# Expert stage of a two-layer backbone: full and small experts in alternating blocks, on one core

## The chip, the cores and the metric

The kernel runs on one core of a Trainium2 chip. The metric is the device time in microseconds, as the median of several executions. A profile of one execution shows where the time goes. The engines are TensorE (PE in the profile, with its weight loads as PEld), VectorE (DVE), ScalarE (ACT), GpSimd (POOL) and SyncE (SP), whose queue issues nearly all loads from HBM.

## The reference, cut to what matters

256 latent and 256 context tokens of width 1024 go through two layers, each with a mixer (gated linear attention, differential attention, neighbourhood attention) and a channel mixer. In the second layer the channel mixer is a mixture of eight experts, computed for the 256 latent tokens. This is the part that changes:

```python
def swiglu(h, wg, wu, wd):
    return (jax.nn.silu(h @ wg) * (h @ wu)) @ wd

def moe_swiglu(h, w_router, wg, wu, wd):
    ...
    logits = (t @ w_router).astype(jnp.float32)
    top_v, top_i = lax.top_k(logits, TOP_K)          # 2 of 8
    top_w = jax.nn.softmax(top_v, axis=-1)
    gates = jnp.sum(jax.nn.one_hot(top_i, N_EXPERTS, dtype=jnp.float32) * top_w[..., None], axis=1)
    y = jnp.zeros_like(t)
    for e in range(N_EXPERTS):
        y = y + gates[:, e:e + 1].astype(t.dtype) * swiglu(t, wg[e], wu[e], wd[e])
    return y.reshape(shp)
```

Everything is float32. An expert has wg and wu of 1024 x 3584 and wd of 3584 x 1024, 44 MB together; all eight are 352 MB, and every one is read once.

## The kernel before, in words

The kernel runs the first layer, then the second layer's mixer, then the expert stage, then the final norm. The tokens of an expert are gathered with one-hot matrices (S) by PE, and its results are scattered back into xtk, the token-major sum, in the same way. Experts are ordered by their token count (`order_experts`, `order_index`); expert 0 stays first, so that its loads can start early. The first four in this order (NBIG) are full: they take up to 128 tokens. The last four are small: up to 64 tokens. A branch at the end does the rest if some expert has more, and is not taken here.

An expert goes in NJ = 7 blocks of 512 hidden columns. A block loads six pieces of 1 MB: two halves of gate, two halves of up, two halves of the down weights of the block before. Between gate and up PE transposes the block before's activations (`g_T`).

*Full experts* (`expert`): the weights are split into a high and a low part (`convert`, lines 789 to 804): ScalarE copies to the rounded format float32r, VectorE subtracts. Each product is then three products (`mm3`: high-high, high-low, low-high) of 128 x 512 columns. Split pieces live in three pairs of buffers (mpr twice, mpc once), used in turn. The raw piece is free once it is split.

*Small experts* (`expert_small`): the raw float32 weights are used as they are (`load_raw`). Two products with 64 token columns each stand side by side in the two halves of the array and of one PSUM bank (gate and up, or the two halves of the down columns). The raw piece is free once PE has used it.

*The ring of slots*: each load takes the next slot of a list (`slot32`). `first` gives the slots of the first loads, `ring` the order after that, and `until` the load number from which a slot is taken out, because its memory then serves as something else. Some slots are memory of tiles that are needed only later (xh, xl: the gathered tokens of experts 2 and 3, xt: xtk, y: the split scatter operand, xc: part of xT). Five slots are left after load 62. SP issues loads in order, and each waits until its slot is free.

*Order*: the Tile framework records the program, fixes the order of instructions on each engine by a priority close to program order, and inserts the semaphores. `plan` hangs smaller jobs behind certain blocks: the ordering of the experts, gathers, one-hot matrices, rows of broadcast vectors, the addition of x. All full experts run first, then all small ones; the `tail` of an expert (its last down product and scatter) runs in the first block of the next.

*PSUM*: pgu has two banks each for the tags pg and pu, pdn one each for pd0 and pd1, pmt two for transposes, gathers and scatters. A small expert uses pg and pu in turn and one of pd0 and pd1.

*Scatter of a full expert* (`scatter_half`, line 1163): y is scaled, split into high and low (ScalarE, VectorE), and two float32r products per token half add up in PSUM.

Of the kernel before, what the change touches and what calls it, by code (L numbers as in the profile page):

```python
# [89 lines left out]
def hybrid_backbone_kernel(  # L90
# [679 lines left out]
    n_load = [0]  # L770

# [81 lines left out]
    tab = const.tile([P, TAB_C], F32, name="tab")  # L853
    nc.sync.dma_start(tab, k_tab[:, 0:TAB_C])
    mskF = const.tile([P, 2, P], U32, name="mskF")
# [31 lines left out]
    for k in range(KD):  # L887
# [10 lines left out]
    pgu = pool("pgu", 2, space=PSUM)  # L898
# [15 lines left out]
    S = mp.tile([P, 2, NE, P], F32R, name="S")  # L914
# [24 lines left out]
    for q in range(2):  # L939
        for t in range(2):  # L940
            pt = pgu.tile([P, 512], F32, tag="pg" if t == 0 else "pu", name="pht")
# [24 lines left out]
    def onehots(e0, n, pos):  # L966
        return tt(S[:, :, e0:e0 + n, :], tb("iota", tab2, TAB_C).rearrange("p (a b n) -> p a b n", a=1, b=1).to_broadcast([P, 2, n, P]),
           pos[:, :, e0:e0 + n].unsqueeze(3).to_broadcast([P, 2, n, P]), ALU.is_equal)

    def onehots_twice():  # L970
        n = NE - NBIG
        it = tb("iota", tab2, TAB_C)[:, 0:P // 2].rearrange("p (a b n) -> p a b n", a=1, b=1).to_broadcast([P, n, 2, P // 2])
        for t in range(2):
            tt(S[:, t, NBIG:NE, :].rearrange("p e (d n) -> p e d n", d=2), it,
               posp[:, t, NBIG:NE].rearrange("p (e a b) -> p e a b", a=1, b=1).to_broadcast([P, n, 2, P // 2]), ALU.is_equal)

    tc.keep_in_program_order(onehots(0, 1, posm))
# [92 lines left out]
    def load_e(dram, kk, n):  # L1070
        i = n_load[0]
        n_load[0] += 1
        wh, wl = ready[i] if i in ready else convert(i, slot32(i), dram, kk, n, (mpr, mpr, mpc)[i % 3])
        return wh.rearrange("p (k n) -> p k n", n=n), wl.rearrange("p (k n) -> p k n", n=n)
# [19 lines left out]
    def gather_small():  # L1094
        n = (NE - NBIG) * (P // 2)
        xs = mp.tile([P, KD, n], F32, tag="xeH1", name="xs")
        for m in range(0, KD, 2):
            pt = bank(pmt, "pga")
            for mi in range(2):
                for i, (src, t) in enumerate(((htH, 0), (htL, 0), (htH, 1), (htL, 1))):  # L1100
                    mm(pt[:, mi * n:(mi + 1) * n], lhsT=src[:, t, (m + mi) * P:(m + mi + 1) * P],
                       rhs=S[:, t, NBIG:NE, 0:P // 2], start=i == 0, stop=i == 3)
# [3 lines left out]
    def gate_up(w_ap, xe, j, tag):  # L1106
        ps = pgu.tile([P, 512], F32, tag=tag, name=tag)
        for half in range(2):
            w = load_e(w_ap[half * 512:(half + 1) * 512, j * 512:(j + 1) * 512].rearrange("(k p) n -> p k n", p=P), 4, 512)
# [5 lines left out]
    def act_mul(pg, pu):  # L1115
        g = mp2.tile([P, 512], F32, tag="eg", name="eg", bufs=2)
# [15 lines left out]
    NJ = FE // 512  # L1132

    def down(w_ap, gt, j, pds):
        for half in range(2):
            w = load_e(w_ap[j * 512 + half * 256:j * 512 + (half + 1) * 256, :].rearrange("(k p) n -> p k n", p=P), 2, D)
# [7 lines left out]
    def down_cols(w_ap, gt, pds, o):  # L1144
        r0 = (NJ - 1) * 512
        w = load_e(w_ap[r0:r0 + 512, o * 512:(o + 1) * 512].rearrange("(k p) n -> p k n", p=P), 4, 512)
        for q in range(4):
            mm3(pds[o], (gt[0][:, q, :], gt[1][:, q, :]), (w[0][:, q, :], w[1][:, q, :]), False, q == 3)

    def scatter_pre(Sf, gate_col):  # L1150
        pt = bank(pmt, "pst")
        for t in range(2):
            nc.tensor.transpose(pt[:, t * P:(t + 1) * P], f32(Sf(t)), ident)
        for t in range(2):
            mm(pt[:, 256:257], lhsT=f32(Sf(t)), rhs=gate_col(t), start=t == 0, stop=t == 1)
        ST = mp2.tile([P, 256], F32R, tag="ST", name="ST", bufs=2)
# [3 lines left out]
        return ST, gs, mp2.tile([P, 2, D], F32R, tag="y", name="yHL")  # L1160

    def scatter_half(sc, pds, o, first=False):
        ST, gs, yHL = sc
        yo = part(y32, o)
        cs = slice(o * 512, (o + 1) * 512)
        yH, yL = yHL[:, 0, cs], yHL[:, 1, cs]
# [12 lines left out]
    def expert(xe, wg, wu, wd, Sf, gate_col, tail, hooks=None, first=False, end=None):  # L1179
        pds = None  # L1180
        prev = None
        for j in range(NJ):
            pg = gate_up(wg, xe, j, "pg")
# [4 lines left out]
            pu = gate_up(wu, xe, j, "pu")  # L1188
            g = act_mul(pg, pu)
            if prev is not None:  # L1190
                if pds is None:
                    pds = [pdn.tile([P, 512], F32, tag=f"pd{o}", name="pd") for o in range(2)]
                down(wd, gt, j - 1, pds)
# [3 lines left out]
            for f in (hooks or {}).get(j, ()):  # L1197
                f()
# [5 lines left out]
        def t1():  # L1204
            if end:
                tc.keep_in_program_order(nc.scalar.preload_act_table_set(LN_EXP))
                sc = scatter_pre(Sf, gate_col)
                new_xg()
                for o in range(2):
                    down_cols(wd, last[0], pds, o)  # L1210
                    scatter_half(sc, pds, o)
                    end(o)
                return
            down(wd, last[0], NJ - 1, pds)
# [3 lines left out]
        return t0, t1  # L1218

# [8 lines left out]
    def expert_small(xs, wg, wu, wd, e, tail, hooks, end=None):  # L1228
# [4 lines left out]
        def g_Ts(g):  # L1233
# [3 lines left out]
            gt = mp2.tile([P, 4, H], F32, tag="gth", name="gts", bufs=2)  # L1237
# [3 lines left out]
        def down_s(gt, j):  # L1241
            if pd[0] is None:
                pd[0] = pdn.tile([P, 512], F32, tag=f"pd{e % 2}", name="pds")
# [9 lines left out]
        for j in range(NJ):  # L1253
            ps = pgu.tile([P, 512], F32, tag=("pg", "pu")[j % 2], name="pgs")
# [13 lines left out]
            g = mp2.tile([P, 512], F32, tag="eg", name="eg", bufs=2)  # L1268
# [7 lines left out]
            for f in (hooks or {}).get(j, ()):  # L1276
                f()
# [5 lines left out]
        def t1():  # L1283
# [3 lines left out]
            down_s(last[0], NJ - 1)  # L1287
            pt = bank(pmt, "pst")
            for t in range(2):
                nc.tensor.transpose(pt[:, t * P:(t + 1) * P], f32(S[:, t, e, :]), ident)  # L1290
            for t in range(2):
                mm(pt[:, 256:257], lhsT=f32(S[:, t, e, :]), rhs=gatp[:, t, e:e + 1], start=t == 0, stop=t == 1)
# [22 lines left out]
    def new_xg():  # L1315
        nonlocal xg
        xg = mp.tile([P, 2, D], F32, tag="xeH0", name="xg")
# [24 lines left out]
    def gather_at(e, n, xe, o=0):  # L1342
        return gather(lambda t: S[:, t, e:e + n, :].rearrange("p e n -> p (e n)"), n * P, xe, o)
# [3 lines left out]
    gather_at(0, 1, x01)  # L1347

    def gather_pair():
        xes[2] = gather_at(2, 2, xe_tiles(0))  # L1350
# [4 lines left out]
    def stack_ga2():  # L1355
        for o in range(2):
# [3 lines left out]
    plan = {(0, 1): [order_experts], (0, 2): [order_index, lambda: onehots(1, 1, posp)], (0, 4): [lambda: gather_at(1, 1, x01, P), load_order],  # L1360
            (0, 6): [lambda: row_bc(ga2b, lambda k: modT[1][:, 40 + k, 0:1])],
# [77 lines left out]
```

## Time and profile before

| | us |
|---|---|
| median of 3 runs (1972.12 to 1978.58) | 1977.36 |
| the profiled execution | 1977.44 |
| its span, first to last instruction | 1975.6 |
| PE busy | 1828.8 (93%) |
| DVE busy | 980.6 (50%) |
| ACT busy | 758.3 (38%) |

The page's slices show the two halves of the expert stage. Each digit is the busy share of a fortieth of the span (49.4 us) in tenths; the expert stage begins near slice 20.

```profile
PE   7999999999999999999899999999999878787886
DVE  5574554633333345755678888988984000010101
ACT  4424454422222234245466777667762000000001
PEclk9999999999999999999899999999999999989998
DMA  9664242342344244633579889999998999999996
GB/s 306 214 173 131 75 143 88 127 129 70 102 131 158 78 126 156 165 116 125 202 283 329 291 292 340 338 349 359 347 339 288 394 394 388 388 366 392 388 388 253
```

From slice 31 on VectorE and ScalarE are nearly idle, PE is below nine tenths, and the DMA moves more than before. Busy times of overlapped products count once; a product's own duration includes the overlap with its neighbours, so the pace of PE is read from the distance of starts.

### The profile page before, as it was taken

The numbers are of one execution on the slowest core, as the hardware profiler recorded it, in microseconds if no ns is written. First come the engines' busy times: TensorE is split into PE (matmuls) and PEld (weight loads), VectorE is DVE, ScalarE is ACT, GpSimd is POOL, SyncE is SP. The second block draws the span as 40 slices with busy tenths as digits, with TensorE's granted clock in tenths as the row PEclk, the third lists the DMA queues.
The fourth block names the chain that finished last, engine by engine and source line by source line (L and its number), as shares of the span: only waits on it lengthen the run. The fifth ranks groups of instructions, "written<-read, shape, count | busy, mean of one in ns | idle before, by whom it ended". The sixth has DMA issues, their size and how long they took to land.

```text
span 1975.6 us, 23201 instructions
## 1 busy us (share of the span) xinstructions
PE 1828.8 (93%) x9152; PEld 1255.2 (64%) x9152; DVE 980.6 (50%) x1296; ACT 758.3 (38%) x967; POOL 46.6 (2%) x75
## 2 busy tenths in 40 slices
PE   7999999999999999999899999999999878787886
PEld 4856766778877878677687878878784222222221
DVE  5574554633333345755678888988984000010101
ACT  4424454422222234245466777667762000000001
POOL 1030000000000000300000000000000000000000
PEclk9999999999999999999899999999999999989998
DMA  9664242342344244633579889999998999999996
GB/s 306 214 173 131 75 143 88 127 129 70 102 131 158 78 126 156 165 116 125 202 283 329 291 292 340 338 349 359 347 339 288 394 394 388 388 366 392 388 388 253
DMA packets 286113, 480.04 MB, mean 243 GB/s; under 512 B 11246, under 2 KB 141612, under 8 KB 285996
## 3 DMA queue, kind: packets, MB, share of 16 engines
q1 hardware_dynamic: 283488, 474.19, 68.2%
q0 software_dynamic: 1312, 2.62, 0.9%
q10 hardware_dynamic: 1196, 1.66, 0.3%
q8 instruction: 74, 1.21, 0.3%
q14 instruction: 43, 0.35, 0.1%
HBM read 477.39 MB, written 1.05 MB: 242 GB/s over the span
## 4 chain that ended last, share of the span: by engine, by line
PE 75%; DMA 13%; DVE 6%; ACT 3%; issue 2%; POOL 0%; DVEq 0%; ACTq 0%; POOLq 0%
DMA e<-in_w_moe_up_dram 12%; PE pd L1141 8%; PE pgs L1261 7%; PE pu L150 3%; PE pds L1249 3%; PE pu L151 3%; PE pg L149 3%; PE pu L149 3%; PE pg L150 3%; PE pg L151 3%; PE psg L149 2%; PE psg L150 2%; PE psg L151 2%; PE psu L149 2%; PE psu L150 2%; PE psd L149 2%
## 5 line engine op out<-in xcount | busy, mean ns | idle before, releaser
L803 DVE TENSOR_TENSOR el<-e,eh 128x2048 fp32r<-128x2048 f32 (+1 forms) x173 | 375.7, 2190 | 50.1 <-ACT eh L802 49.4
L802 ACT ACTIVATE eh<-e 128x2048 fp32r<-128x2048 f32 (+1 forms) x173 | 316.3, 1837 | 95.7 <-PE pu L151 33.7
L1261 PE MATMUL pgs<-e,xs 128*64 128x512 f32 x896 | 244.7, 623 | 75.1 <-DMA e<-in_w_moe_up_dram 69.8
L1261 PEld LDWEIGHTS pgs<-e,xs 128*64 128x64 f32 x896 | 70.2, 141 | 235.1 <-DMA e<-in_w_moe_up_dram 110.4
L142 ACT ACTIVATE wh<-w 128x2048 fp32r<-128x2048 f32 (+2 forms) x70 | 125.4, 1791 | 205.6 <-issue 78.6
L143 DVE TENSOR_TENSOR wl<-w,wh 128x2048 fp32r<-128x2048 f32 (+2 forms) x70 | 149.6, 2138 | 99.1 <-ACT wh L142 99.1
L1270 DVE TENSOR_TENSOR eg<-eg,pgs 64x512 f32<-64x512 f32 x28 | 19.3, 690 | 359.7 <-ACT eg L1269 359.7
L1269 ACT ACTIVATE eg<-pgs 64x512 f32<-64x512 f32 x28 | 16.5, 590 | 372.2 <-PE pgs L1261 372.2
L1249 PE MATMUL pds<-e,gts 128*64 128x512 f32 x448 | 127.6, 600 | 1.4 <-DMA e<-in_w_moe_down_dram 1.4
L149 PE MATMUL pg<-eh,xeH 128*128 128x512 f32 x224 | 89.9, 402 | 0.6 <-ACT eh L802 0.6
L150 PE MATMUL pg<-el,xeH 128*128 128x512 f32 x224 | 90.0, 402 | 0.0
L150 PE MATMUL pu<-el,xeH 128*128 128x512 f32 x224 | 89.3, 399 | 0.7 <-DVE el L803 0.6
L149 PE MATMUL pu<-eh,xeH 128*128 128x512 f32 x224 | 89.7, 401 | 0.0
L149 PE MATMUL psp<-hH,wh 128*128 128x512 f32 (+1 forms) x224 | 86.4, 390 | 3.1 <-ACT hH L274 3.0
L151 PE MATMUL pg<-eh,xeL 128*128 128x512 f32 x224 | 89.0, 397 | 0.0
L149 PE MATMUL psq<-wh,hH 128*128 128x256 f32 x304 | 88.7, 292 | 0.0
L151 PE MATMUL pu<-eh,xeL 128*128 128x512 f32 x224 | 88.5, 395 | 0.0
L150 PE MATMUL psq<-wl,hH 128*128 128x256 f32 x304 | 87.7, 289 | 0.0
L151 PE MATMUL psq<-wh,hL 128*128 128x256 f32 x304 | 87.4, 287 | 0.0
L150 PE MATMUL psp<-hL,wh 128*128 128x512 f32 (+1 forms) x224 | 85.8, 383 | 0.0
L151 PE MATMUL psp<-hH,wl 128*128 128x512 f32 (+1 forms) x224 | 85.2, 381 | 0.0
L1141 PE MATMUL pd<-el,gth 128*128 128x512 f32 x224 | 71.5, 400 | 1.6 <-DVE el L803 1.6
(504 smaller groups left out, 3436.3 us busy)
## 6 DMA issues: line engine op xcount, KB each, us to landing
e<-in_w_moe_gate_dram SPq DMA_DIRECT2D x111, 1024.0 KB, 7.8
e<-in_w_moe_up_dram SPq DMA_DIRECT2D x111, 1024.0 KB, 7.7
e<-in_w_moe_down_dram SPq DMA_DIRECT2D x111, 1024.0 KB, 7.6
wmod<-in_w_mod_dram SPq DMA_DIRECT2D x96, 512.0 KB, 5.4
w<-in_w_in_dram SPq DMA_DIRECT2D x24, 1024.0 KB, 8.0
w<-in_w_ffn_gate_dram SPq DMA_DIRECT2D x11, 1024.0 KB, 5.9
w<-in_w_ffn_up_dram SPq DMA_DIRECT2D x11, 1024.0 KB, 5.1
w<-in_w_out_dram SPq DMA_DIRECT2D x8, 1024.0 KB, 5.3
```

What stands on the lines that cost most here:

```text
L142: act(wh[:, :m], w32[:, :m], AF.Copy)
L143: tt(wl[:, :m], w32[:, :m], f32(wh[:, :m]), ALU.subtract)
L149: mm(ps, lhsT=sh, rhs=mh, start=first, stop=False)
L150: mm(ps, lhsT=sh, rhs=ml, start=False, stop=False)
L151: mm(ps, lhsT=sl, rhs=mh, start=False, stop=last)
L802: act(h3[:, b], w[:, b], AF.Copy)
L803: tt(l3[:, b], w[:, b], f32(h3[:, b]), ALU.subtract)
L1141: mm(pds[o], lhsT=gt[sh][:, q, :], rhs=w[mh][:, k, o * 512:(o + 1) * 512], start=a and j == 0 and q == 0, stop=z and j == NJ - 1 and q == 3)
L1249: mm(pd[0][H * o:H * o + H, :], lhsT=gt[:, q, :], rhs=w[:, k, o * 512:(o + 1) * 512], start=j == 0 and q == 0, stop=j == NJ - 1 and q == 3 ...
L1261: mm(ps[H * o:H * o + H, :], lhsT=xv[:, kk, :], rhs=ws[o][:, k, :], start=kk == 0, stop=kk == KD - 1, skip_group_check=True)
L1269: act(g[0:H], ps[0:H], AF.Silu)
L1270: tt(g[0:H], g[0:H], ps[H:P], ALU.mult)
```

## The change

- Full and small blocks alternate. `full_ones` and `small_ones` are generators that yield after each block; a loop runs one full block, then one small block, the small ones starting LAG = 4 blocks later. So four full blocks come first, 24 pairs follow, and four small blocks come last.
- `Weights` keeps the list of a full expert's loads through all four experts. After each full block it issues and splits AHEAD = 3 loads of the next one, ahead of the small block's loads in program order.
- The ring has a new slot v, and y stays in it: eight slots are left after load 42.
- The memory comes from the one-hot matrices, now built per expert (`onehot`, tile S1, two buffers) instead of for all eight, from the split scatter operand, from the buffers of eg, and from tab and mskF, which move from the pool const to a pool that is closed before the expert stage.
- Experts 2 and 3 are gathered one by one into the halves of experts 0 and 1 (x01), instead of together.
- A full expert's scatter multiplies the float32 y in one product instead of its two halves in two.
- PSUM: pgu has one bank each for pg, pu and the small experts' ps; pdn one each for pd0, pd1 and the small experts' pds.
- The jobs of `plan` hang behind blocks by number (`after`).

```diff
-    tab = const.tile([P, TAB_C], F32, name="tab")
+    tabp = big.enter_context(tc.tile_pool(name="tabp", bufs=1))
+    tab = tabp.tile([P, TAB_C], F32, name="tab")
...
-    pgu = pool("pgu", 2, space=PSUM)
+    pgu = pool("pgu", 1, space=PSUM)
...
+             "v": lambda: mp2.tile([P, 2048], F32, tag="v32", name="e32"),
...
-    first = ["r0", "r1", "r2", "w", "c", "r0", "r1", "xh", "xl", "xt", "y", "r2", "xc"]
-    ring = ["w", "c", "r0", "r1", "xh", "xl", "xt", "y", "r2", "xc"]
-    until = {"xc": 36, "xt": 42, "y": 42, "xh": 62, "xl": 62}
+    first = ["r0", "r1", "r2", "w", "c", "r0", "r1", "xh", "xl", "xt", "y", "v", "r2", "xc"]
+    ring = ["w", "c", "r0", "r1", "xh", "xl", "xt", "y", "v", "r2", "xc"]
+    until = {"xc": 26, "xt": 42, "xh": 22}
...
+    def onehot(pos, e, n=P):
+        S = mp2.tile([P, 2, P], F32R, tag="S1", name="S", bufs=2)
...
+    AHEAD = 3
...
+    class Weights:
+        def __init__(self, experts):
+            self.todo, self.got = [], []
+            for i, (wg, wu, wd) in enumerate(experts):
+                for j in range(NJ):
+                    for w_ap in (wg, wu):
+                        self.todo += [(w_ap, j, h) for h in range(2)]
+                    if j or i:
+                        self.todo += [((wd if j else experts[i - 1][2]), (j - 1) % NJ, h + 2) for h in range(2)]
+            self.todo += [(experts[-1][2], NJ - 1, h + 2) for h in range(2)]
+        def fetch(self, n):
+            while self.todo and len(self.got) < n:
+                w_ap, j, h = self.todo.pop(0)
...
+                self.got.append(load_e(ap.rearrange("(k p) n -> p k n", p=P), kk, m))
+        def next(self):
+            self.fetch(1)
+            return self.got.pop(0)
...
     def scatter_half(sc, pds, o, first=False):
...
-        act(half(yH), yo, AF.Copy)
-        tt(half(yL), yo, half(f32(yH)), ALU.subtract)
         for t in range(2):
             py = bank(pmt, "py")
-            mm(py, lhsT=ST[:, t * P:(t + 1) * P], rhs=yH, start=True, stop=False)
-            mm(py, lhsT=ST[:, t * P:(t + 1) * P], rhs=yL, start=False, stop=True)
+            mm(py, lhsT=ST[:, t * P:(t + 1) * P], rhs=yo, start=True, stop=True)
...
     def expert(...)
...
             prev = g
+            ws.fetch(AHEAD)
+            yield
...
+    LAG = 4
...
+    after = {0: [order_experts], 1: [order_index], 3: [gather_rest, load_order],
+             4: [lambda: row_bc(ga2b, lambda k: modT[1][:, 40 + k, 0:1])],
+             5: [lambda: gather_at(1, x01, P)],
+             8: [add_x], 9: [stack_ga2], 10: [lambda: gather_at(2, x01, 0)], 17: [lambda: gather_at(3, x01, P)],
+             16: [lambda: row_bc(gfb, lambda k: gfT[:, k:k + 1])]}
+    bigs, smalls = full_ones(), small_ones()
+    for i in range(NBIG * NJ + LAG):
+        next(bigs, None)
+        if i >= LAG:
+            next(smalls, None)
+        for f in after.get(i, ()):
+            f()
+    next(smalls, None)
     finish()
```

## Rows read from the trace of the kernel before

**Rows 1.** Windows: stretch, length, busy PE, PEld, DVE, ACT, POOL; clock, DMA share, GB/s.

```profile
1250.00:1300.00 50.00, 49.92 (x226) 40.05 (x225) 46.37 (x33) 34.74 (x24) 0.00 (x0) 1.00 0.97 345
1400.00:1450.00 50.00, 49.98 (x231) 40.77 (x230) 41.54 (x23) 35.74 (x25) 0.00 (x0) 1.00 1.00 358
1550.00:1600.00 50.00, 39.56 (x166) 12.45 (x166) 2.92 (x5) 2.53 (x5) 0.00 (x0) 1.00 1.04 394
```

**Rows 2.** Chain of waits in order of time: start us, length us, what.

```profile
1031.52 5.45 PE pd L1141 x24
1048.61 5.47 PE pd L1141 x24
1065.72 5.48 PE pd L1141 x24
1088.65 5.45 PE pd L1141 x24
1587.75 3.22 PE pgs L1261 x13
1593.15 10.53 DMA e<-in_w_moe_up_dram
1603.72 3.22 PE pgs L1261 x13
1948.65 8.75 DMA e<-in_w_moe_down_dram
```

**Rows 3.** What SP's queue waited for: us in total, times, longest us.

```profile
SPq L796 <- DVE el L803: 380.7, 140, 16.5
SPq L1225 <- PE pgs L1261: 247.9, 101, 10.5
```

**Rows 4.** Timeline of PE's weight loads and transposes in a small block.

```profile
1572.28 0.14 PEld L1261 LDWEIGHTS pgs<-e,xs 128*64 128x64 f32 x2 [0.28 <-issue]
1572.71 0.14 PEld L1261 LDWEIGHTS pgs<-e,xs 128*64 128x64 f32 x2 [0.28 <-issue]
1577.09 0.46 PE L1236 MATMUL pgt<-ident,eg 64*128 64x64 f32 x4
```

**Rows 5.** Groups by line, from 1000 us on: busy us, mean ns, idle before.

```profile
L803 DVE TENSOR_TENSOR el<-e,eh 128x2048 fp32r<-128x2048 f32 (+1 forms) x165 | 366.1, 2237 | 44.7 <-ACT eh L802 44.0
L1261 PE MATMUL pgs<-e,xs 128*64 128x512 f32 x896 | 244.7, 623 | 75.1 <-DMA e<-in_w_moe_up_dram 69.8 <-DMA e<-in_w_moe_gate_dram 5.1
L1249 PE MATMUL pds<-e,gts 128*64 128x512 f32 x448 | 127.6, 600 | 1.4 <-DMA e<-in_w_moe_down_dram 1.4
L802 ACT ACTIVATE eh<-e 128x2048 fp32r<-128x2048 f32 (+1 forms) x163 | 306.1, 1885 | 90.3 <-PE pu L151 33.7 <-PE pd L1141 30.6 <-PE pg L151 22.8
```

**Rows 6.** Shorter windows within the full experts, columns as in rows 1.

```profile
1050.00:1070.00 20.00, 20.00 (x90) 16.30 (x90) 18.81 (x13) 14.56 (x10) 0.00 (x0) 1.00 1.05 384
1382.00:1386.00 4.00, 4.00 (x19) 3.25 (x18) 3.77 (x4) 2.52 (x3) 0.00 (x0) 1.00 1.02 340
```

**Rows 7.** Loads of the page: size, median us from issue to landing.

```profile
e<-in_w_moe_up_dram SPq DMA_DIRECT2D x111, 1024.0 KB, 7.7
```

**Rows 8.** Timelines of SP and PE, and tile tab: min/median/max ns, first start.

```profile
32.64 2.86 SPq L854 DMA_DIRECT2D tab<-in_k_tab_dram x1
50.71 1.06 PE L229 MATMUL psmod<-wmod,Sz 128*32 128x256 f32 x14
L440 DVE TENSOR_TENSOR gu<-psu,tab x16: 681/684/692, 93.8 to 816.1; 128x512 f32<-128x512 f32 x16
```

**Rows 9.** PE's timeline where full experts give way to small ones.

```profile
1506.81 0.73 PE L1141 MATMUL pd<-eh,gth 128*128 128x512 f32 x2 [2.48 <-ACT eh L802]
1509.13 1.22 PE L1141 MATMUL pd<-el,gth 128*128 128x512 f32 x2 [1.59 <-DVE el L803]
1511.01 1.05 PE L1141 MATMUL pd<-eh,gth 128*128 128x512 f32 x2
```

**Rows 10.** The window around that place.

```profile
1491.00:1530.00 39.00, 34.92 (x130) 15.67 (x128) 12.58 (x16) 7.02 (x8) 0.00 (x0) 0.91 0.75 272
```

More of the change, by code (lines that the diff above doesn't have):

```diff
@@ L770, in hybrid_backbone_kernel @@
     n_load = [0]
+    n_conv = [0]
     wr = tab2 = None
@@ L1130, in g_T, with down @@
         return gh, gl
-    NJ = FE // 512
-    def down(w_ap, gt, j, pds):
+    def down(ws, gt, j, pds):
         for half in range(2):
-            w = load_e(w_ap[j * 512 + half * 256:j * 512 + (half + 1) * 256, :].rearrange("(k p) n -> p k n", p=P), 2, D)
+            w = ws.next()
             for k in range(2):
@@ L1177, in scatter_half, with expert @@
                 tt(xtk[:, t, cs], xtk[:, t, cs], py, ALU.add)
-    def expert(xe, wg, wu, wd, Sf, gate_col, tail, hooks=None, first=False, end=None):
+    def expert(xe, ws, Sf, gate_col, tail, first=False):
         pds = None
@@ L1204, in t1 @@
         def t1():
[L1205 to L1214, printed above, removed]
+            down(ws, last[0], NJ - 1, pds)
             sc = scatter_pre(Sf, gate_col)
@@ L1218, in expert, with run_expert @@
         return t0, t1
+    def run_expert(*args):
+        g = expert(*args)
+        while True:
+            try:
+                next(g)
+            except StopIteration as stop:
+                return stop.value
     def load_raw(dram, kk, n):
@@ L1226, in load_raw, with expert_small @@
         return wv
-    def expert_small(xs, wg, wu, wd, e, tail, hooks, end=None):
+    def expert_small(xs, wg, wu, wd, e, tail, end=None):
         H = P // 2
@@ L1275, in expert_small @@
             prev = g
-            for f in (hooks or {}).get(j, ()):
-                f()
+            yield
         last = []
@@ L1366, in hybrid_backbone_kernel @@
-    tail = None
-    for e in range(NE):
-        if e == 0:
-            ws = [w[0, 0] for w in (wm_g, wm_u, wm_d)]
-        else:
-            ws = [w[0, ds(which[e], 1)].rearrange("o a b -> (o a) b") for w in (wm_g, wm_u, wm_d)]
-        hooks = {j: f for (ee, j), f in plan.items() if ee == e}
-        if e >= NBIG:
-            tail = expert_small(xes[NBIG], *ws, e, tail, hooks, square if e == NE - 1 else None)
-            continue
-        xe, h = (x01, e * P) if e < 2 else (xes[2], (e - 2) * P)
-        xv = (xe[0][:, :, h:h + P], xe[1][:, :, h:h + P])
-        gt_ = gates if e == 0 else gatp
-        tail = expert(xv, *ws, lambda t, e=e: S[:, t, e, :], lambda t, e=e, g=gt_: g[:, t, e:e + 1], tail, hooks, e == 0)
@@ L1380, in hybrid_backbone_kernel, with weights, full_ones @@
-    tail[0]()
-    tail[1]()
+    LAG = 4
+    def weights(e):
+        if e == 0:
+            return [w[0, 0] for w in (wm_g, wm_u, wm_d)]
+        return [w[0, ds(which[e], 1)].rearrange("o a b -> (o a) b") for w in (wm_g, wm_u, wm_d)]
+    def full_ones():
+        tail = None
+        ws = Weights([[lambda e=e, i=i: weights(e)[i] for i in range(3)] for e in range(NBIG)])
+        for e in range(NBIG):
+            h = e % 2 * P
+            xv = (x01[0][:, :, h:h + P], x01[1][:, :, h:h + P])
+            gt_, ps_ = (gates, posm) if e == 0 else (gatp, posp)
+            tail = yield from expert(xv, ws, lambda e=e, p=ps_: onehot(p, e)[0], lambda t, e=e, g=gt_: g[:, t, e:e + 1], tail, e == 0)
+        tail[0]()
+        tail[1]()
@@ new lines, in small_ones @@
+    def small_ones():
+        tail = None
+        for e in range(NBIG, NE):
+            tail = yield from expert_small(xes[NBIG], *weights(e), e, tail, square if e == NE - 1 else None)
+        tail[0]()
+        tail[1]()
+    after = {0: [order_experts], 1: [order_index], 3: [gather_rest, load_order],
[3 more added lines that the diff above has]
+             16: [lambda: row_bc(gfb, lambda k: gfT[:, k:k + 1])]}
```

100 lines of the change are left out of this document (46 added, 54 removed).

## The prediction, made before the result was known

> **What bounds the kernel now.** I read the slices of the page first, then the windows of the last half, the chain of waits, the queue's own waits and the groups by line. The expert stage begins at about 990 us and has two halves. In the first, four full experts run in 28 blocks: PE is busy 49.9 to 50 us of every 50, VectorE 42 to 46, and the DMA delivers 345 to 358 GB/s [rows 1]. In the second, four small experts run in 28 blocks: PE is busy 40 of 50, VectorE 3, and the DMA is full at 394 GB/s [rows 1]. The chain says the same: a full block comes every 17.09 us (1031.52 to 1048.61, the down products of two neighbours) with no wait in it, a small block every 15.96 us (1587.75 to 1603.72, the gate and up products) with a DMA wait in each [rows 2]. Both kinds load six pieces of 1 MB, so a piece takes 2.85 us where PE sets the pace and 2.66 us where the DMA does. SP's queue waits on VectorE's split in the first half and on PE's products in the second [rows 3]: there the loads wait for a slot, since the first half cannot use more and the second has only five slots left. So the first half lacks PE, the second lacks DMA, and neither lends its spare to the other. The clock was granted at 2.4 GHz through the first half.
>
> **What a round costs after the change.** A round is one full and one small block. PE in the full block: 17.1 us. PE in the small block: weight loads come in twos 0.43 us apart where nothing holds them [rows 4]; 896 and 448 products in 28 blocks [rows 5] are 32 and 16 each, so 16 x 0.43 + 8 x 0.43 = 10.3 us, and 0.5 for four transposes: 10.8 us. Together 27.9 us. DMA: 12 pieces, at 2.66 us 31.9 us. VectorE: six splits of 2.24 us [rows 5] and four shorter operations of about 0.7: 16.2 us; ScalarE less. So a round is bound by the DMA, with 4 us of PE to spare, and the stage is 336 pieces at the DMA's pace. Before, only 28 of the 56 blocks ran at it.
>
> Do eight slots keep the queue full? In a round 12 pieces pass 8 slots, so at 2.70 us a piece a slot may be held 21.6 us from issue to release. I walked one round slot by slot: a piece lands 2.70 after the one before; a full piece is split 4.1 us after landing (ScalarE 1.9, VectorE 2.2, [rows 5]), and only when the piece three before it has been used, since there are three pairs of split buffers; a small piece is freed when PE has used it. From landing to release that is about 10.6 us for a full piece and 5 for a small one, 8 in the mean, which leaves 13 us from issue to landing; the page's median landing is 7.7 [rows 7]. So the queue holds about two pieces to spare, and short PE stalls (up to about 5 us) do not reach the DMA. The three pieces of the next full block that are split ahead of the small block change nothing in this sum: they let PE begin the full block without the 4.1 us of a split, which PE has to spare. They add one wait: the third of these splits cannot begin before PE has ended the full block, and behind it on ScalarE stand the small block's copies and Silu. PE first needs those 7 us into the small block, the split is through after 4.1, so nobody waits for them.
>
> **The rate.** The trace of before never shows the mix. The nearest rows: with PE and VectorE both full, but several pieces queued (share 1.05), 20 us gave 384 GB/s; a short window with a share of 1.02 gave only 340, right after the queue had run low [rows 6]. The small half gave 394. Bounds: 2.66 us (small blocks) and 2.85 us (full blocks). I take 2.70 us (388 GB/s), between the 384 of a full queue beside full engines, which this ring keeps, and the 394 beside small blocks.
>
> **The sum.** Up to the fourth full block nothing is interleaved and PE sets the pace as before: its down products end at 1048.61 + 5.47 = 1054 us. 22 pieces are used by then, and with nine slots (eight, and xtk's until piece 42) and three split ahead 34 have landed by about 1061. The ring is full while the small gather runs, so I let the DMA idle 7 us: next landing at 1071. From there 301 pieces x 2.70 = 813 us: 1884. The gather of expert 1 (1065.72 to 1088.65, 22.9 us between down products instead of 17.1) can drain the ring once more: +4. The small half of before had 28 x 15.96 = 447 us of loads and took about 7 more at its three changes of expert; I leave 6 of it: last landing 1894. Before, the last piece landed at 1957.4 and the span ended at 1975.6 [rows 2]; the tail of 18.2 us is the same code: 1912. Around the span lie 1977.44 - 1975.6 = 1.8 us: 1914, rounded to **1915 us**, 62 less than before. The profiled execution stands at the median (1977.36), so nothing is shifted. At 2.66 the same sum is 1903, at 2.85 it is 1960.
>
> **The smaller edits**, all beside the DMA:
> - Small blocks' gate and up now share one PSUM bank, full blocks' pg and pu one each. Silu and the multiply take 0.6 and 0.7 us and the next use of the bank comes a block later: nothing. In the first four blocks the distance is still a down product, 5.5 us.
> - The one gather for experts 2 and 3 becomes two. Expert 1's cost 22.9 - 17.1 = 5.8 us of PE [rows 2], so one more is at most 6 us, out of 24 x 4 us to spare. If PE were the bound it would be these 6 us.
> - One-hot tiles per expert: 0.42 us of VectorE each, eleven in all, against about 2.5 us taken out; VectorE is half idle in a round.
> - Scatter of a full expert: the split of y (0.6 on ScalarE, 0.7 on VectorE per half) goes, and four pairs of products at 0.23 us become four f32 ones. At the f32 row rate above (two for 0.43) they cost between 0.43 and 0.86 each: 0 to 1.6 us per expert, hidden like the gathers.
> - tab and mskF move to a pool opened where the first loads lay. SP issues them at 32.6 us; the last product on those loads ends at about 52 [rows 8]. If SP stood there, six wmod and two w pieces queued behind it would be late by up to 19 us, where PE now hardly waits; if the load is merely put later, nothing, since tab is first read at 93.8 us [rows 8] and mskF later still. The pool could also give a load an earlier place, -1. I take 0 and keep +10 for the range.
> - Reading the experts' order into SP's registers now comes before the first small load. The numbers are ready two blocks earlier, as before: nothing, or up to one small load's 2.7 us if SP has to wait.
>
> **Rivals.**
> 1. *The DMA is slower beside the splits.* For it: in the first half a share of 0.97 to 1.00 went with only 345 to 358 GB/s [rows 1]. Against: rows 6, where it reached 384 under the same load. At 345 GB/s (3.04 us) for the 17 us of a full block and 2.66 for the rest, a piece takes 2.85 in the mean: 1960. At the 358 GB/s of the last full window throughout, 2.93 us, it is 1984. The Trainium skill's page "SBUF — State Buffer", section "Summary: rules for kernel authors", says to reckon loads from HBM at about 358 GB/s; by that figure the sum would be the same 1984. The trace of the small half, 394 GB/s over 50 us, goes against that rule on this core.
> 2. *PE's order of instructions stalls the round* (the slower side). Where before went over from full to small, small products stood in PE's queue among the full expert's down products: PE waited 2.48 and 1.59 us for a split, then ran at the lower clock, 1.2 GHz (four products from 1509.13 to 1511.01, 1.88 us; at the pace of [rows 2], 24 in 5.46, they take 0.91) [rows 9], and over 39 us the DMA fell to 272 GB/s [rows 10]: 12 us lost. After the change every round has two such changes. If each round lost 3 us of DMA, 24 x 3 = 72 us, the result would be 1987. It decides from 62 / 24 = 2.6 us per round on. Against: at that place PE was the only user of five slots; now the queue holds some 5 us in reserve, and the split weights stand ready.
> 3. *The ring leaks a little:* 1 us of DMA idle per round, and tab late: 1915 + 24 + 10 = 1949.
> 4. *The change doesn't interleave:* if the emitted order put small blocks after the full ones, 1977. The order on an engine stays close to that of the program, and here the program order itself alternates.
>
> **How the numbers follow.** Forecast (1895 to 1935): 0.66. Rivals 1 and 3 (1935 to 1971): 0.20. No change (rival 4, or rival 1 or 2 ending near 1977): 0.03. Rival 2, or rival 1 at 358 GB/s throughout, slower: 0.09. Below 1895: 0.02. A change under 0.3% (6 us) cannot be told from none. Faster: 0.66 + 0.20 + 0.02 = 0.88, same 0.03, slower 0.09. The range goes from the sum at 2.66 less the 6 us for changes of expert (1897) to the sum at 2.85: 1897 to 1960.
>
> **What would show it.** Between about 1090 and 1840 us the DMA share at 1.03 or more and 380 to 394 GB/s in every window; down products of full blocks 32 to 33 us apart; PE about 87% busy with waits on landings; SP's waits on both splits and small products. Wrong: a DMA share below 1.0 in mid-stage (rival 2 or 3: then PE's waits are on splits and the clock falls), a full share with 350 GB/s (rival 1), or PE waiting for w before 100 us (tab).

## The result, and the profile after

The change makes the kernel slower: 2021.21 us (median of 4 runs, 2018.44 to 2024.87) against 1977.04 for the kernel before in the same session (1972.12 to 1978.58). The ratio is 1.0224, with an interval of 1.0211 to 1.0237. The forecast was 1915 us, 1897 to 1960; the result lies 61 us above the range. The profiled execution has a span of 2017.5 us.

The stretches of [rows 1] in the windows of the changed kernel (length, busy PE, PEld, DVE, ACT, POOL, then granted clock, DMA share, GB/s):

```profile
1250.00:1300.00 50.00, 49.12 (x212) 32.27 (x211) 26.59 (x20) 19.94 (x16) 0.00 (x0) 0.95 0.94 340
1400.00:1450.00 50.00, 49.06 (x196) 29.12 (x197) 29.81 (x24) 18.53 (x12) 0.00 (x0) 0.98 0.92 344
1550.00:1600.00 50.00, 47.71 (x196) 29.94 (x196) 27.31 (x21) 18.91 (x14) 0.00 (x0) 0.97 0.96 359
```

The blocks do alternate: none of these windows has VectorE at 46 of 50 us, and none has it at 3. But the DMA share is below 1.0 in each, and PE is busy 47 to 49 of 50. By the prediction's own last paragraph that is rival 2 or 3, not rival 1. PE is busier than before while less gets done: the page counts 1894.2 us of busy PE, 65 more than before, for the same products but for the scatters. The question is what fills PE. The start of two full blocks in PE's timeline gives the length of a round:

```profile
1592.13 0.39 PE L149 MATMUL pg<-eh,xeH 128*128 128x512 f32 x1
...
1629.35 0.39 PE L149 MATMUL pg<-eh,xeH 128*128 128x512 f32 x1
```

37.2 us (36.1 in the mean of the 22 rounds from 1088.6 us on), where 32 were forecast. What PE (for products) and SP's queue waited for (us in total, times, longest us; the PE rows are for 1060 to 1850 us, the SP rows are for the whole run and answer to [rows 3]):

```profile
PE pu L150 <- DVE el L804: 32.4, 19, 2.8
PE pu L149 <- ACT eh L803: 14.2, 7, 2.3
...
SPq L1243 <- DVE el L804: 261.4, 91, 9.0
...
SPq L797 <- PE pgs L1279: 232.1, 82, 6.7
```

In this stretch PE has no wait for a landing of weights. It waits for splits, and nearly always in the same place, at the up products of a full block (pu). The timeline around one such place shows why (all engines, lines in between left out):

```profile
1388.40 0.59 ACT L1287 ACTIVATE es<-pgs 64x512 f32<-64x512 f32 x1 [10.72 <-PE pgs L1279]
...
1392.39 0.38 ACT L287 ACTIVATE gts<-pgt 128x256 f32<-128x256 f32 x1 [3.40 <-PE pds L1267]
1392.67 5.50 ACT L803 ACTIVATE eh<-e 128x2048 fp32r<-128x2048 f32 x3
...
1394.62 0.77 PE L149 MATMUL pu<-eh,xeH 128*128 128x512 f32 x1 [2.28 <-ACT eh L803]
1396.95 0.80 PE L150 MATMUL pu<-el,xeH 128*128 128x512 f32 x1 [1.56 <-DVE el L804]
...
1398.39 0.63 PE L150 MATMUL pu<-el,xeH 128*128 128x512 f32 x1
1398.82 0.63 PE L151 MATMUL pu<-eh,xeL 128*128 128x512 f32 x1
```

The split of the fourth piece (eh, L803) stands in ScalarE's queue behind two instructions of the small block. The first is es, its Silu, which waits 10.72 us for the small block's last gate or up product. The second is gts, the copy of the activations just made, which the next small block needs and the emitted order brings forward; it waits 3.40 us more for the last down products, since they read the one buffer that it writes. The full block's gate products and the first half of its up products were emitted ahead of the small block or among its products. So when the small block ends, PE has only the second half of pu in front of it, whose split has just begun: it waits 2.28 and 1.56 us. Then it runs at the lower clock (granted 0.50, 1.2 GHz, from 1397.6 to 1401.5 us), products 0.43 us apart instead of 0.23. The Trainium skill's page "PSUM — Partial Sum Buffer", section "Engine vs sequencer instructions", says that ScalarE works its queue strictly in order and that PE's products keep theirs; this trace agrees (three splits stood behind the Silu and the copy, and then ran without a wait).

The copies gts go to ScalarE and VectorE by turns; on VectorE they stand ahead of the second part of the split (el). Of the 46.6 us of waits at pu, 34.1 come where gts is the last waiting instruction ahead of the split, 1.9 (two rounds) where it is the Silu alone, and 10.6 where it is another small job (add_x, a row of broadcasts, a gather, a scatter).

The second loss shows in PE's timeline as pgs x2: one small product that runs singly. (A float32 product is two records, so a pair for the two column halves is four.)

```profile
1525.10 0.40 PE L150 MATMUL pg<-el,xeH 128*128 128x512 f32 x1
1525.42 1.07 PE L1279 MATMUL pgs<-e,xs 128*64 128x512 f32 x2
1526.42 0.50 PE L151 MATMUL pg<-eh,xeL 128*128 128x512 f32 x1
1526.76 0.40 PE L149 MATMUL pu<-eh,xeH 128*128 128x512 f32 x1
...
1528.93 3.65 PE L1279 MATMUL pgs<-e,xs 128*64 128x512 f32 x14
```

The single product takes 1.00 us from start to start. By [rows 4] a pair takes 0.86. The seven products left over hold a second single one, so their 14 records last 3.58 us to the next start (median of 24 such runs) instead of 2.99. From 1060 to 1830 us there are 39 runs of two records. A broken pair thus costs 0.57 + 0.59 = 1.16 us of small products. The full products on both sides of the single one lose 0.1 us each besides (0.32 and 0.34 us to the next start instead of 0.23). The groups that answer to [rows 5] (busy us, mean ns, idle before):

```profile
L804 DVE TENSOR_TENSOR el<-e,eh 128x2048 fp32r<-128x2048 f32 (+1 forms) x174 | 376.2, 2188 | 67.9 <-ACT eh L803 67.2
...
L1279 PE MATMUL pgs<-e,xs 128*64 128x512 f32 x896 | 254.1, 601 | 6.6 <-DMA e<-in_w_moe_up_dram 6.4
```

### The profile page after: what moved, and what is told of

The parts are those of the page before. It is cut to its first block, busy times and chain, and to the rows that moved or that the text cites. A ratio compares the mean times of both kernels' runs of the same rounds, so it can differ in the third digit from the quotient of the medians.

```text
span 2017.5 us, 23212 instructions
## 1 busy us (share of the span) xinstructions
PE 1894.2 (94%) x9184; PEld 1266.0 (63%) x9184; DVE 975.6 (48%) x1300; ACT 749.8 (37%) x963; POOL 46.6 (2%) x75
## 5 line engine op out<-in xcount | busy, mean ns | idle before, releaser
L803 ACT ACTIVATE eh<-e 128x2048 fp32r<-128x2048 f32 (+1 forms) x174 | 313.6, 1833 | 123.1 <-PE pu L151 77.8
L1279 PE MATMUL pgs<-e,xs 128*64 128x512 f32 x896 | 254.1, 601 | 6.6 <-DMA e<-in_w_moe_up_dram 6.4
L1288 DVE TENSOR_TENSOR es<-es,pgs 64x512 f32<-64x512 f32 x28 | 19.3, 690 | 306.6 <-ACT es L1287 306.6
L150 PE MATMUL pu<-el,xeH 128*128 128x512 f32 x224 | 102.3, 457 | 34.6 <-DVE el L804 34.6
L1287 ACT ACTIVATE es<-pgs 64x512 f32<-64x512 f32 x28 | 16.5, 590 | 293.0 <-PE pgs L1279 293.0
L1267 PE MATMUL pds<-e,gts 128*64 128x512 f32 x448 | 122.9, 599 | 0.5 <-DVE gts L289 0.5
L149 PE MATMUL pu<-eh,xeH 128*128 128x512 f32 x224 | 101.6, 454 | 16.5 <-ACT eh L803 16.5
L151 PE MATMUL pu<-eh,xeL 128*128 128x512 f32 x224 | 99.3, 444 | 0.0
L150 PEld LDWEIGHTS pu<-el,xeH 128*128 128x128 f32 x224 | 48.2, 215 | 55.1 <-DVE el L804 41.3
```

The lines of the kernel that those rows point to most:

```text
L149: mm(ps, lhsT=sh, rhs=mh, start=first, stop=False)
L150: mm(ps, lhsT=sh, rhs=ml, start=False, stop=False)
L151: mm(ps, lhsT=sl, rhs=mh, start=False, stop=last)
L803: act(h3[:, b], w[:, b], AF.Copy)
L1267: mm(pd[0][H * o:H * o + H, :], lhsT=gt[:, q, :], rhs=w[:, k, o * 512:(o + 1) * 512], start=j == 0 and q == 0, stop=j == NJ - 1 and q == 3 ...
L1279: mm(ps[H * o:H * o + H, :], lhsT=xv[:, kk, :], rhs=ws[o][:, k, :], start=kk == 0, stop=kk == KD - 1, skip_group_check=True)
```

## The experiments

The times (medians; ratio to the kernel before of the same session, with its interval):

| kernel | us | ratio |
|---|---|---|
| the change | 2021.2 | 1.0224 [1.0211, 1.0237] |
| e1 lag 28 (no interleaving) | 1972.7 | 0.9971 [0.9958, 0.9984] |
| e2 PE held to program order | 1909.9 | 0.9663 [0.9640, 0.9686] |
| e3 nothing split ahead | 1982.3 | 1.0027 [1.0008, 1.0045] |
| e4 held, small block in the middle | 1914.4 | 0.9690 [0.9667, 0.9714] |
| e5 late Silu, PE free | 1941.5 | 0.9814 [0.9783, 0.9846] |
| e6 held, nothing split ahead | 1953.1 | 0.9875 [0.9839, 0.9912] |
| e7 held, half of the small bytes | 1889.7 | 0.9563 [0.9530, 0.9595] |
| e8 held, pairs among the down products | 1976.4 | 0.9990 [0.9972, 1.0008] |
| e9 held, half of the small products | 1900.0 | 0.9606 [0.9583, 0.9629] |
| e10 held and late Silu | 2039.4 | 1.0316 [1.0287, 1.0345] |
| e11 held, lag 3 | 1916.7 | 0.9690 [0.9661, 0.9720] |
| e12 whole pairs, PE free | 1973.6 | 0.9976 [0.9962, 0.9989] |
| e13 whole pairs and late Silu, PE free | 1911.5 | 0.9670 [0.9653, 0.9688] |

Theory A: the order in which PE and ScalarE get the instructions of the two kinds costs the time. Rivals: the DMA is slower beside splits (B), or one of the smaller edits costs it (C).

**e1, no interleaving.**

```diff
-    LAG = 4
+    LAG = 28
```

> All 28 full blocks first, then all 28 small ones (the lag of the small blocks is 28 instead of 4); every other edit of the change stays: the scatter in f32, gathers one by one, one PSUM bank each, tab's new place, three pieces split ahead. Theory A (the loss comes from how full and small instructions are mixed on PE and ScalarE): 1968 to 1985 us, level with before, since the stage is then before's two halves. Rival B (the DMA is slower beside splits): also level with before, since its halves are unmixed. Rival C (one of the other edits costs the time): 2005 to 2025, as slow as the change.

1972.7 us, level with before or 0.3% better. So the smaller edits together cost nothing that shows (rival C falls): the loss is in the alternation.

**e2, PE held to program order.** `keep_in_program_order` puts an instruction behind the one recorded before it on its engine. Products and transposes of the expert stage go through it.

```diff
-    mm = nc.tensor.matmul
+    strict = [False]
+    def pin(i):
+        return tc.keep_in_program_order(i) if strict[0] else i
+    def mm(*a, **k):
+        return pin(nc.tensor.matmul(*a, **k))
...
     bigs, smalls = full_ones(), small_ones()
+    strict[0] = True
```

> The change with one edit: PE's products and transposes of the expert stage are held to the order in which the program writes them, so a full block's 16 gate and up products are no longer brought forward among the small block's. Theory A (PE's order): 1915 to 1940 us, rounds of 32 to 33 us, DMA share above 1.0, no products at 0.43 us pace in the full block. Rival B (DMA slower in the mix): 2000 to 2020, windows still at 345 to 360 GB/s with PE waiting on landings. Rival C (other edits): about 2020.

1909.9 us, 111 less than the change, and 5 below the 1915 us that were both the forecast and the lower end of what theory A gave. No work is added or taken away. The same three windows:

```profile
1250.00:1300.00 50.00, 49.82 (x235) 33.12 (x233) 32.17 (x23) 25.18 (x20) 0.00 (x0) 1.00 1.04 397
1400.00:1450.00 50.00, 50.00 (x230) 30.88 (x227) 23.96 (x15) 21.92 (x17) 0.00 (x0) 1.00 1.04 397
1550.00:1600.00 50.00, 50.00 (x228) 29.57 (x227) 26.98 (x18) 21.31 (x16) 0.00 (x0) 1.00 1.04 390
```

The DMA gives 390 to 397 GB/s beside the splits of the mix and a full PE: rival B, the prediction's rival 1, is refuted for this mix (VectorE is busy 24 to 32 of 50 us in it, 42 to 46 in the full half of before).

**e3, nothing split ahead** (`AHEAD = 0`).

> The change with no piece of the next full block split ahead of the small block (0 instead of 3); the blocks still alternate. With nothing split ahead, the first products of a full block are ready only after the small block, so they cannot be brought forward. Theory A: faster than the change, 1930 to 1965 us, with a short wait on a split at the head of each full block. Rival B: 2000 to 2025. Rival D (the split ahead does help, as the change means it): slower than the change, 2030 to 2060, each of 24 rounds longer by one split of about 4 us less what covers it.

1982.3 us: 39 faster than the change, so rival D falls for this order, but short of the 1930 to 1965 expected. The wait only moved, from the fourth split to the first two of a full block (PE, 1060 to 1850 us):

```profile
PE pg L150 <- DVE el L804: 31.3, 20, 2.8
PE pg L149 <- ACT eh L803: 14.4, 8, 2.3
```

These 45.7 us are nearly the 46.6 of the change. What fell are the broken pairs: 19 runs of two records from 1060 to 1830 us instead of 39.

**e4, the small block in the middle.** PE held as in e2; the full block yields, and has three pieces split ahead, between gate and up.

> As the held order, but the small block is written between the gate and the up products of a full block instead of between two full blocks, so the splits that follow it have more PE work in front of them. Theory A: 1910 to 1945 us, within 15 of the held order. Rival B: 2000 to 2020, and the held order the same. If the number of changes between full and 64-column products on PE sets the time (2 to 3 per round here against about 8 in the change), both held orders lie together near 1930.

1914.4 us, within 5 of e2. Where the small block stands matters little once the order is held.

**e5, late Silu.**

```diff
-            act(g[0:H], ps[0:H], AF.Silu)
-            tt(g[0:H], g[0:H], ps[H:P], ALU.mult)
             if prev is not None:
                 down_s(gt, j - 1)
...
             yield
+            g = mp2.tile([P, 512], F32, tag="es", name="es")
+            tc.keep_in_program_order(act(g[0:H], ps[0:H], AF.Silu))
+            tt(g[0:H], g[0:H], ps[H:P], ALU.mult)
```

> The change with one edit: on ScalarE the Silu of a small block stands behind the splits of the next full block instead of ahead of them (PE's order is left free, and in the emitted order small and full products stay mixed). Theory A1 (the loss is mostly PE waiting for splits that stand behind a Silu, which itself waits for PE: 54 us more stalls and 23 us more at the lower clock between 1060 us and the last down product than in the held order): 1935 to 1965 us. Theory A2 (it is mostly the changes between full and 64-column products on PE): 1995 to 2020, still over 100 switches and 25 us or more for them.

1941.5 us, within theory A1's 1935 to 1965 and 80 less than the change, with PE's mixing left nearly as it was (37 runs of two records). The edit moves the Silu and, with it, all that needs it: the multiply, the transposes and the copy gts. PE's waits at pu on splits of the low part fall from 32.4 us to

```profile
PE pu L150 <- DVE el L804: 5.6, 6, 2.8
```

and those on the high part (14.2 us) are gone. So the cost of what the small block puts in front of the splits is shown. The run does not divide it between the Silu and the copy; by the waits of the change, the copy has the larger part.

**e6, held, nothing split ahead.**

> The held order with no piece split ahead of the small block. By the prediction (the three pieces split ahead change nothing in the sum): 1904 to 1918 us. Rival (each of 24 rounds then starts with a wait for a split of 4.1 us, less the 3.4 us of small down products that cover it, and a piece is freed later): 1925 to 1960, DMA share below 1.0 in mid-stage.

1953.1 us, within the rival's 1925 to 1960 and 43 more than e2: the prediction's "change nothing in this sum" is wrong. PE waits 20.0 us for first splits (16 times), which e2 does not have, and the clock falls after them (17 us lost to it, reckoned as in the table below, instead of 4). So splitting ahead gains 43 us in the held order and loses 39 in the free one (e3), where it is what lets full products be brought forward.

**e7, held, half of the small bytes**, and **e9, held, half of the small products.**

```diff
-        nc.sync.dma_start(wv, dram)
+        nc.sync.dma_start(wv[:, 0:kk // 2], dram[:, 0:kk // 2])
```

```diff
-                for k in range(4):
+                for k in (0, 2):
```

(e7 reads the first half twice; e9 does likewise with one of two down products.)

> The held order, but a small block's six loads bring only half of each piece (0.5 MB instead of 1), and the products read that half twice, so the output is not the reference's. PE's, ScalarE's and VectorE's work is the same. Theory B1 (the DMA sets the pace of the held order, 32 us a round against about 28 of PE): 24 rounds x 3.6 us less and the four small blocks at the end shorter: 1800 to 1835 us. Theory B2 (PE, busy 47.5 of 50 us in the windows, sets it): 1890 to 1910.

> The held order with half of the small block's gate, up and down products left out (one of two for each piece, so every load is still waited for and used; the output is not the reference's). PE has 5.2 us less per round, the loads are all there. With half the bytes the held order took 1890 us, so PE alone needs nearly the whole time. If the DMA's 12 pieces of 2.65 us (31.8 us a round) are the bound beside it: 1885 to 1910 us. If PE alone sets the pace: 20 us less than 1890 x or lower, 1780 to 1860, with the DMA share below 1.0.

1889.7 and 1900.0 us. With a quarter less to load the held order gains only 20 us, and with nearly a fifth less for PE only 10: PE and DMA are nearly balanced in e2, and of e7's two expectations 1800 to 1835 (DMA alone) was wrong and 1890 to 1910 (PE) right; e9 lies in its 1885 to 1910 (DMA). PE's timeline of e7 has a round with nothing else in it:

```profile
1565.17 0.50 PE L107 MATMUL pg<-eh,xeH 128*128 128x512 f32 x1
...
1582.39 3.65 PE L107 MATMUL pgs<-e,xs 128*64 128x512 f32 x16
...
1589.85 3.60 PE L107 MATMUL pds<-e,gts 128*64 128x512 f32 x16
1593.38 0.50 PE L107 MATMUL pg<-eh,xeH 128*128 128x512 f32 x1
```

28.2 us; 27.9 were forecast. (In the held kernels all products have one line, that of the helper.) But over 22 rounds, from 1089.1 to 1780.3, the mean is 31.4: a round with a gather has 4.5 us more, one with a scatter 7 to 9. Here is the scatter of a small expert in e2's timeline; PE stands idle in it, and the next products are 0.43 us apart:

```profile
1531.14 0.50 PE L107 MATMUL pst<-gatp,S 128*128 128x1 f32 x4
1533.32 1.13 PE L107 MATMUL py<-xT,STs 64*128 64x512 f32 x4 [1.67 <-DVE xT L1326]
1535.19 2.67 PE L107 MATMUL py<-xT,STs 64*128 64x512 f32 x4 [0.75 <-DVE xtk L1335]
...
1538.81 0.63 PE L107 MATMUL pg<-eh,xeL 128*128 128x512 f32 x1
1539.23 0.63 PE L107 MATMUL pg<-eh,xeH 128*128 128x512 f32 x1
```

e9's windows show the DMA alone, share 1.04 throughout:

```profile
1250.00:1300.00 50.00, 42.74 (x188) 26.45 (x186) 28.37 (x21) 21.39 (x19) 0.00 (x0) 1.00 1.04 398
...
1550.00:1600.00 50.00, 44.05 (x188) 27.63 (x188) 27.04 (x17) 23.00 (x18) 0.00 (x0) 1.00 1.04 399
```

**e8, held, pairs among the down products.** After every six down products of a full block the program gives two of the small block's gate and up products.

```diff
                     for o in range(2):
                         mm(pds[o], lhsT=gt[sh][:, q, :], rhs=w[mh][:, k, o * 512:(o + 1) * 512],
...
+                if mixed[0]:
+                    next(mixed[0], None)
```

> The held order, written so that the first eight gate and up products of the small block stand in four pairs among the full block's 24 down products (6 pd, 2 pgs, four times over): three more runs of 64-column products per round, no other work and no new wait on a split. In the change a run of two takes 1.00 us where two in a row of them take 0.43, 0.57 more. If that price holds, PE gets 3 x 0.57 = 1.7 us more per round: 1908 to 1922 if the DMA still sets the pace, 1935 to 1955 if PE does. If the changes are free: 1904 to 1914 and the pairs take 0.43 to 0.5 us.

1976.4 us, more than either theory said. A whole pair among full products takes 1.01 us from start to start (0.86 in a row of pairs), and the full product on either side of it loses 0.1 us:

```profile
1560.75 0.63 PE L107 MATMUL pd<-el,gth 128*128 128x512 f32 x2
1561.22 0.63 PE L107 MATMUL pd<-eh,gtl 128*128 128x512 f32 x2
1561.78 1.08 PE L107 MATMUL pgs<-e,xs 128*64 128x512 f32 x4
1562.79 0.74 PE L107 MATMUL pd<-eh,gth 128*128 128x512 f32 x2
1563.36 0.63 PE L107 MATMUL pd<-el,gth 128*128 128x512 f32 x2
```

From 1561.22 to 1563.36 pass 2.14 us; four full products and a pair at their pace take 1.79. So a change to 64 columns and back costs 0.35 us, not 0.57, and 72 such pairs some 26 us. The Trainium skill's page "TensorEngine Tiling (Array Packing)", section "Key Properties", says that a change of tiling mode drains PE; a price on each change agrees with that, but no run shows the drain itself. The rest is a wait I had not counted: the small block's pieces are held longer, and PE now waits for landings, 32 us in all (pds 18.0, pgs 10.0 and 4.0, from 1060 to 1850 us). The two make 58 of the 66 us that e8 takes more than e2.

**e10, held and late Silu** (e2's and e5's edits).

> The held order and the Silu of a small block behind the splits of the next full block. If in the held order no split that PE needs stands behind that Silu any more (PE has its gate products and half of its up products in front): 1905 to 1915 us, no difference. If part of the 11 rounds longer than 30 us comes from it: 1890 to 1903.

2039.4 us, the slowest of all, and neither expectation. One row of PE's waits (1060 to 1850 us) tells why:

```profile
PE pgs L107 <- DVE es L1303: 85.8, 17, 5.1
```

The small blocks have one PSUM bank for gate and up. In the held order the next small block begins right after the full block, but the late Silu, which empties that bank, stands behind a split that waits for the full block's last products. Free, PE fills this with products brought forward; held, it waits 5 us in each of 17 rounds. The prediction costed the single bank at nothing; with the Silu in its early place that holds.

**e11, held, lag 3.**

> The held order with the small blocks one block earlier (lag 3 instead of 4; the small gather one block earlier, and the ring gives up xeH0 at piece 16 instead of 22). Between 991 and 1075 us the held order's DMA moved 246 to 335 GB/s against 395 later; one more round instead of a block at either end saves the DMA's idle time of one full block at the start, 1.3 us, and part of the drop at the small gather and at the end: 1898 to 1912 us. If the ring with one slot less early starves the gather: 1912 to 1920.

1916.7 us, inside the interval for a starved ring, and not better than e2. It gives nothing to carry on.

**e12 and e13, whole pairs**, without and with e5's edit. The two products of a pair change places, and the second is held behind the first, so that it never waits for a piece of its own.

```diff
-                    for o in range(2):
-                        mm(ps[H * o:H * o + H, :], ...
+                    for o in (1, 0):
+                        i_ = mm(ps[H * o:H * o + H, :], ...
+                        if o == 0:
+                            tc.keep_in_program_order(i_)
```

> The change with one edit: of the two products of a small block that use the two halves of PE's columns, the up one is issued first and the gate one is held behind it, so no product of a pair runs alone; ScalarE's order and the mixing of full and small products stay. In the change a single product takes 1.00 us and the run of seven that it leaves behind 3.58, 1.16 us more per broken pair than whole pairs. If that is the price: 24 to 39 broken pairs, 28 to 45 us less than 2021, 1976 to 1995 us. If PE then only waits longer for the split behind the Silu: 2008 to 2021.

> Both edits, the late Silu and the pairs, with PE's order free otherwise. If the 31 us that the late Silu alone leaves to the held order are broken pairs: 1905 to 1920 us. If they come from the mixing itself: 1930 to 1945. Below 1905 only if the free order also takes the waits out of the scatters that the held order has (7 scatters with 2 to 4 us of waits each) and the DMA is not the bound then.

e12: 1973.6 us, 48 less than the change and 2 below the expected 1976 to 1995. The waits and the busy time of the small gate and up products (e12, 1060 to 1850 us for the waits):

```profile
PE pu L150 <- DVE el L804: 32.7, 19, 2.8
PE pu L149 <- ACT eh L803: 14.2, 7, 2.3
...
L1279 PE MATMUL pgs<-e,xs 128*64 128x512 f32 x896 | 206.9, 605 | 8.1 <-DMA e<-in_w_moe_up_dram 8.1
```

The waits are those of the change to 0.3 us; the busy time falls from 254.1 to 206.9 us, 47 us, and that is the gain. (No run of two records is left among the full products, so changes of mode went together with the broken pairs.) e13, with both edits: 1911.5 us, within its 1905 to 1920 and level with the held order, though full and small products are still mixed. Its windows:

```profile
1250.00:1300.00 50.00, 49.22 (x230) 30.22 (x230) 27.99 (x21) 23.85 (x18) 0.00 (x0) 1.00 1.04 399
1400.00:1450.00 50.00, 48.30 (x218) 26.76 (x217) 23.05 (x16) 19.84 (x15) 0.00 (x0) 1.00 1.04 400
```

e2 and e13 beat the kernel before by 3.4 and 3.3% and cannot be told apart.

## Why the prediction was wrong

PE's time from 1060 us to the last down product of a full expert, added up from the starts in the timelines. A product is reckoned at 0.2335 us (gate, up), 0.2275 (down) or 0.2133 per record (small); what it took beyond that is put down to a wait where there is one, else to the clock (full products over 1.5 times their pace) or to changes of mode and broken pairs. Waits that follow a transpose, a gather or a scatter are in the last row (some 17 us in e2, 6 in the change):

| us | change | e12 pairs | e5 late Silu | e13 both | e2 held |
|---|---|---|---|---|---|
| PE idle after a product | 59.2 | 58.3 | 14.4 | 27.4 | 5.6 |
| changes of mode, broken pairs | 75.4 | 21.5 | 64.8 | 24.2 | 19.9 |
| lower clock | 26.6 | 32.7 | 8.0 | 3.8 | 3.5 |
| products at pace; transposes, gathers, scatters | 710.5 | 707.5 | 713.6 | 714.1 | 734.5 |
| sum | 871.7 | 820.0 | 800.8 | 769.5 | 763.5 |

- **The step that failed** is in "What a round costs": the slot walk and its "nobody waits for them" took PE to run each block in the order of the program, with "The order on an engine stays close to that of the program" as the ground (rival 4) and "the split weights stand ready" as the reason against rival 2. The emitted order is not that one: ready full products go ahead of the small block, the fourth split stays behind the Silu and the copy that follows it, and pairs are torn apart. So the 27.9 us of PE in a round became 36.1. Held to the program's order, the same instructions take 1909.9 us.
- **Its two causes are shown.** Late Silu (with the copy) alone: 80 us. Whole pairs alone: 48. Both: 110 of the 111 us that the held order gains. They add up to more (128), which fits a floor: with half of the small bytes the held order still takes 1890 us (e7), and with half of the small products 1900 (e9).
- **Rival 2** named the right mechanism (a stall on a split, then the lower clock, twice a round), and [rows 9] showed both in the kernel before. At 1987 us its price was 34 us too low, since it lacked the broken pairs (the trace of before has a single product too, from 1498.97 to 1499.97 us, 1.00 us, just ahead of [rows 9]); by its own price of 3 us a round the waits and the clock (85.8 us, 3.6 in each of 24 rounds) were nearly right. I gave it 0.09 with rival 1 because the queue held 5 us in reserve; but the reserve is the DMA's, and the lost time was PE's.
- **The DMA's rate**: 2.70 us a piece was a little long. At 398 GB/s (e9) 1 MB takes 2.63, and the sum would be 1894. That the held order lies only 5 us from 1915 is in part luck: the faster DMA makes up for a reserve of PE that is not there. The Trainium skill's page "SBUF — State Buffer", section "Summary: rules for kernel authors", would have one reckon with 358 GB/s; e2, e9 and e13 exceed it in each window shown here (390 to 400).
- **PE's round**: 27.9 forecast, 28.2 measured in a plain round. The "4 us of PE to spare" is not there in the mean (31.4 with gathers and scatters): the scatters' waits were left out. This did not decide the result, but it made the three pieces split ahead worth 43 us in the held order (e6), where the prediction gave them nothing.
- **The smaller edits** together cost nothing that shows (e1). Of tab: SP issues it at 41.73 instead of 32.64 us, it is first read at 94.0 instead of 93.8, and the expert stage begins at 993.8 instead of 989.34 (991.5 to 997.3 in the other kernels with the edit). Some 2 to 8 us may be its price; no run separates it.

Why the emitted order brings full products forward at all stays open. Without pieces split ahead it does so far less (e3), but no run shows by what it decides.

## What to carry to other kernels

When two streams of work are interleaved, write down the order that each engine will really get, its queue included, before reckoning with idle time: an instruction that waits for the end of one stream (here a Silu and a copy) blocks everything of the other stream behind it on its engine. A gain that rests on an order is only there if the order is held; two small edits, or holding PE to the program, turned 2.2% slower into more than 3% faster without any change of the work. And an edit that helps in one order can hurt in the other: splitting ahead (+39 and -43 us) and the late Silu (-80 and +130) both changed sign.

## What the runs showed that I had not expected

- A single 64-column product takes 1.00 us between full products, a pair 1.01: the second half of the columns is nearly free, and a torn pair costs 1.16 us of small products.
- The DMA gave 390 to 400 GB/s beside a PE that was busy 48 to 50 of 50 us and splits on both other engines (e2, e13). That the 345 to 358 of [rows 1] were the pace of PE fits this and the 384 of [rows 6], but no run of the mix has VectorE at the 42 to 46 us of that half.
- e8: 0.35 us for a change to 64-column products and back.
- A copy of 0.4 us that the emitted order brought forward held up more of the splits than the Silu itself (34.1 and 1.9 us of PE's waits).
